# GpSimd's elementwise work given to VectorE and ScalarE: weight splits, the head, the recurrent branch, the gates and the feed-forward products by sevens

## The chip, the cores and the metric

The kernel runs on one core of one Trainium2 chip. The core has TensorE (PE in the profile; PEld is its weight load), VectorE (DVE), ScalarE (ACT), GpSimd (POOL) and SyncE (SP, which here only issues DMAs). The metric is device microseconds for one execution of the whole program: the median of three runs before was 2143.12 us. Lower is better.

## The reference, cut to what matters

One layer of a hybrid decoder trunk on one sequence of 1024 tokens, width 1024, all in float32:

```
h = rmsnorm(x);  proj = h @ w_in                     # 1024 x (2048 + 1544 + 1792 + 3072)
ya = spatial gating MLP (gelu, layernorm, causal mix of 128-token chunks)
yb = forgetting attention (8 heads of 64, softmax with a decay from a cumulated log-sigmoid)
yc = RWKV-7 time mixing (8 heads of 64; token shift, low-rank decay/gates, recurrent state,
     group norm, bonus)
gates = sigmoid(proj[:, gate columns] + bias)        # three of width 1024
x = x + (gates0*(ya@p_a) + gates1*(yb@p_b) + gates2*(yc@p_c)) @ w_out
h = rmsnorm(x);  x = x + (silu(h @ w_gate) * (h @ w_up)) @ w_down      # inner width 2816
out = rmsnorm(x)
```

## The kernel before

**Split products.** Every large matmul is done in a reduced-precision float format by splitting each operand into two tiles: `hi`, a rounded copy that ScalarE writes (`nc.scalar.copy`, a CAST), and `lo`, the remainder `raw - hi` that another engine subtracts. `mm3` (L154 to L158) then issues three matmuls for each block: hi*hi, hi*lo, lo*hi. So each weight tile needs one CAST and one subtraction before the TensorE can use it, and each activation too. The subtraction for weights stands in `w_split` (L134, subtraction on L139); its engine is `low[0]`, which before is GpSimd for the whole program.

**Products by sevens.** Two stages (the gates, about 77 to 325 us of the profile, and the feed-forward up products, about 1530 to 1905 us) use class `Seven` (L317): blocks of a 2x2 product are made from seven products instead of eight (Strassen-Winograd). For each step `f` of such a stage, `begin` does two products from split weights `w_hi`, `w_lo`; `sums` adds and subtracts four quarter blocks of weights on VectorE (L367, L368, L370, L375) and `prepared` (L338) splits five results into `o_hi` (ScalarE, L335) and `o_lo` (GpSimd, L336); `rest` does five more products and adds them up on VectorE (L382 to L390). The activation side is likewise summed and split once, into `T1` to `T4`, `B22` (`T_hi`, `T_lo` of 128x512 each). In the feed-forward stage `act_done` multiplies the two halves of the SwiGLU (L747, GpSimd). All small tiles of a stage share one ring of buffers, `piece` (22 and 25 deep).

**The head** (0 to 77 us) normalises `x` in two halves of 512 tokens, transposes it on TensorE and writes, for the first half, `h_hi` (ScalarE), `h_lo` (VectorE) and their sum `b` (GpSimd, L499, 128x512). For the second half it writes `b` only (ScalarE, L501), forms differences (`t2` and others: L504, L505 on VectorE, L506 and L516 on GpSimd), and splits them into the `T` operands. The first gate products need these operands.

**The recurrent branch** (425 to 875 us) runs eight units of the RWKV recurrence as small dependent steps on all engines (`begin`, `finish`, `chain`); between the steps it places parts of large projections (`projections`, whose weights go through `w_split`) so that TensorE has something to do. A triangular inverse is eliminated in 62 small VectorE instructions in a row for each unit (L1217, L1219). GpSimd does `x_lo`, `y_lo` (L1102, L1206, L1330) and half of `kb` (L1123), besides `w_lo` and some DMA issues.

Then follow attention (to 1200 us; GpSimd makes its bias tiles `lg`, L1481, L1482), the chunk mixing of branch a with the projection of b (to 1275 us; `ya_lo`, `y_lo` on GpSimd), the projection of a (to 1425 us), the output projection and second norm (to 1530 us), the feed-forward up products (to 1905 us) and the down products (to the end; no GpSimd work there).

**What sets the order.** The program's text is handed to a scheduler that places the instructions of each engine in one fixed queue; a queue waits at its head for semaphores and nothing overtakes. Tiles come from pools with a given number of buffers, and a writer waits until the reader of the old content is done.

Of the kernel before, what the change touches and what calls it, by code (L numbers as in the profile page):

```python
# [63 lines left out]
def kernel(ctx: ExitStack, tc: tile.TileContext, a: dict, out: bass.AP):  # L64
# [254 lines left out]
    class Seven:  # L319
# [36 lines left out]

        def sums(self, f, g, scratch=()):
# [9 lines left out]
            nc.vector.tensor_tensor(s1, A21, A22, ALU.add)  # L367
# [91 lines left out]
    fetched.append(gs.fetch(1))
    load_x(1, 4)  # L460
    b11, b21, b12, b22, t2, t3 = ([None] * 4 for _ in range(6))
    for half in range(2):
        xi = x_in[half]
# [14 lines left out]
        for b in (0, 2, 1, 3):  # L478
            for q in range(4):
# [3 lines left out]
                else:  # L483
                    nc.vector.tensor_scalar(xt, xt, r[:, q:q + 1], None, op0=ALU.mult)
        if half == 0:

            ops0 = gs.sums(0, fetched[0][0], [h22_tile(i, F32).rearrange("p (a b) -> p a b", a=4) for i in range(5)])
        for k in range(4):
            for kt in (k, 4 + k):
                ps = xps.tile([P, HALF], F32, name="ps_t", tag="t")  # L490
                for q in range(4):
                    nc.tensor.transpose(ps[:, q * P:(q + 1) * P], xi[q // 2, kt // 2][:, q % 2, (kt % 2) * P:(kt % 2 + 1) * P], ident)
                b = gs.piece("b")
                ((b11, b12), (b21, b22))[kt // 4][half][k] = b
                if half == 0:
                    hi, lo = hh(kt, 0)
                    nc.scalar.activation(hi, ps, AF.Copy, scale=pc("norm_mix", kt))
                    nc.vector.scalar_tensor_tensor(lo, ps, pc("norm_mix", kt), hi.bitcast(F32), op0=ALU.mult, op1=ALU.subtract)
                    nc.gpsimd.tensor_tensor(b, hi.bitcast(F32), lo.bitcast(F32), ALU.add)  # L499
                else:  # L500
                    nc.scalar.activation(b, ps, AF.Copy, scale=pc("norm_mix", kt))  # L501
# [6 lines left out]
        if half == 0:  # L508
            begun = [gs.begin(0, fetched[0])]
            first = [next(ops0)]  # L510
    begun.append(gs.begin(1, fetched[1]))
    for T, src in ((T3, b12), (T1, b11)):
        for k in range(4):
            gs.split(T[k], src[k], nc.vector)
            if T is T3:
                nc.gpsimd.tensor_tensor(b21[k], b21[k], t2[k], ALU.subtract)  # L516
    first += [next(ops0) for _ in range(2)]
# [34 lines left out]
    with ExitStack() as st:  # L552
# [13 lines left out]
        low_rank(1, wts)  # L566
        wa_p, g_p = parts("wa", wa_up, nc.gpsimd), parts("g", g_up, nc.gpsimd)
        for half in range(2):
# [4 lines left out]
            for hp in range(4):  # L573
# [430 lines left out]
def rwkv_branch(tc, a, e):  # L1004
# [4 lines left out]
    with ExitStack() as st:  # L1009
# [67 lines left out]
        def begin(n, u):  # L1077
# [43 lines left out]
            for h, hs in enumerate(heads):  # L1121
                nc.vector.tensor_tensor(kb[hs, :, h, :], v3(k)[hs], v3(pi)[hs], ALU.mult)
                nc.gpsimd.tensor_tensor(kb[hs, :, 1 - h, :], v3(av)[hs], v3(pi)[hs], ALU.mult)  # L1123
            yield 1.5
# [407 lines left out]
```

## Time and profile before

| | before |
|---|---|
| median of three runs (lowest, highest) | 2143.12 us (2140.16, 2145.07) |
| the profiled execution, own time / span | 2139.3 us / 2137.4 us |
| granted TensorE clock, mean | 0.967 |
| busy: PE / DVE / ACT / POOL | 94% / 59% / 41% / 39% |
| largest POOL groups | `w_lo` L139 271.1 us in 114, `o_lo` L336 150.8 us in 105 and 90.5 us in 70 |

In the profile a row of a group reads: line, engine, operation, output<-input, shape, count, busy time in us, mean ns of one, then the idle time of the engine just before them and what ended it. A row of waits reads: who waited, for whom, us in total, how many times, the longest.

### The profile page before, as it was taken

To read this page: it belongs to the slowest core of one execution; us is meant where nothing else is said; L and a number is where in the kernel's file an instruction comes from. 1 tells how busy PE (TensorE), PEld (TensorE's weight loads), DVE (VectorE), ACT (ScalarE), POOL (GpSimd) and SP (SyncE) were. 2 spreads that over 40 slices of the span, in tenths; PEclk is the share of its full clock that TensorE was granted. 3 is DMA by queue.
4 is the path that set the end of the run, shared out by engine and by line. 5 is a ranking of instruction groups with operands and counts; after the bars stand their busy time and mean duration, and the time that the engine had idled before them with its cause. 6 is when DMAs were issued, how large, how long until landed. Compare 5 with 4: busy or idle time off the path is not lost. (4 is left out here: it accounts for less than half of the span.)

```text
span 2137.4 us, 31459 instructions
## 1 busy us (share of the span) xinstructions
PE 2000.8 (94%) x11773; PEld 1598.6 (75%) x11773; DVE 1260.3 (59%) x2398; ACT 882.2 (41%) x1566; POOL 824.2 (39%) x630
## 2 busy tenths in 40 slices
PE   5899999899889899899999989998999999999998
PEld 4688886676777667777666668897778887878886
DVE  8754454777677764245466594436655444556966
ACT  6433335334454454357554322245323222224435
POOL 5654451223232232233444432344676666530000
PEclk8899999899999999999899999999999999999999
DMA  4233335333233322543343753443232332349433
GB/s 124 84 112 116 116 102 195 108 92 107 83 111 93 94 81 80 171 116 99 104 125 102 274 180 99 129 154 98 79 111 90 115 99 91 107 158 327 135 99 123
DMA packets 254700, 260.91 MB, mean 122 GB/s; under 512 B 21430, under 2 KB 195588, under 8 KB 254548
## 3 DMA queue, kind: packets, MB, share of 16 engines
q1 hardware_dynamic: 218388, 208.53, 31.1%
q10 hardware_dynamic: 32928, 41.16, 6.0%
q0 software_dynamic: 3232, 9.21, 1.6%
q8 instruction: 92, 1.51, 0.3%
q14 instruction: 60, 0.49, 0.1%
HBM read 176.77 MB, written 77.89 MB: 119 GB/s over the span
## 5 line engine op out<-in xcount | busy, mean ns | idle before, releaser
L139 POOL TENSOR_TENSOR w_lo<-w_raw,w_hi 128x1024 fp32r<-128x1024 f32 (+2 forms) x114 | 271.1, 2380 | 438.9 <-ACT w_hi L138 438.6
L156 PE MATMUL ps_f<-T_hi,o_hi 128*128 128x512 f32 x576 | 226.7, 394 | 8.4 <-ACT o_hi L335 5.9
L157 PE MATMUL ps_f<-T_lo,o_hi 128*128 128x512 f32 x576 | 227.2, 394 | 7.4 <-DVE T_lo L336 7.4
L158 PE MATMUL ps_f<-T_hi,o_lo 128*128 128x512 f32 x576 | 226.1, 393 | 0.4 <-POOL o_lo L336 0.4
L336 POOL TENSOR_TENSOR o_lo<-s,o_hi 128x512 fp32r<-128x512 f32 x105 | 150.8, 1436 | 85.1 <-ACT o_hi L335 79.1
L138 ACT CAST w_hi<-w_raw 128x1024 fp32r<-128x1024 f32 (+2 forms) x114 | 112.6, 989 | 138.2 <-PE ps_p L157 30.0
L156 PEld LDWEIGHTS ps_f<-T_hi,o_hi 128*128 128x128 f32 x576 | 109.1, 189 | 34.2 <-ACT o_hi L335 6.3
L157 PEld LDWEIGHTS ps_f<-T_lo,o_hi 128*128 128x128 f32 x576 | 109.2, 190 | 32.5 <-DVE T_lo L336 9.4
L158 PEld LDWEIGHTS ps_f<-T_hi,o_lo 128*128 128x128 f32 x576 | 109.3, 190 | 24.0 <-POOL o_lo L336 0.8
L157 PE MATMUL ps_d<-w_lo,a_hi 128*128 128x512 f32 x272 | 106.7, 392 | 1.7 <-DVE w_lo L947 1.7
L158 PE MATMUL ps_d<-w_hi,a_lo 128*128 128x512 f32 x272 | 106.7, 392 | 0.0
L156 PE MATMUL ps_d<-w_hi,a_hi 128*128 128x512 f32 x272 | 104.7, 392 | 0.0
L335 ACT CAST o_hi<-s 128x512 fp32r<-128x512 f32 x105 | 65.0, 619 | 94.2 <-DVE s L368 45.8
L367 DVE TENSOR_TENSOR s<-up_raw 128x512 f32<-128x512 f32 x35 | 27.9, 797 | 126.1 <-DMA up_raw<-in_w_gate_up_dram 118.2
L336 POOL TENSOR_TENSOR o_lo<-up_raw,o_hi 128x512 fp32r<-128x512 f32 x70 | 90.5, 1293 | 27.0 <-ACT o_hi L335 15.6
L375 DVE TENSOR_TENSOR s<-w_raw,s 128x512 f32<-128x512 f32 x35 | 60.3, 1724 | 59.9 <-POOL o_lo L336 59.9
L1481 POOL TENSOR_SCALAR lg<-ck,cq 128x128 f32<-128x128 f32 (+7 forms) x64 | 50.4, 788 | 100.9 <-PE tp L1495 95.5
L871 ACT CAST a_hi<-a_raw 128x1024 fp32r<-128x1024 f32 (+1 forms) x42 | 41.2, 981 | 110.9 <-PE ps_d L157 92.3
L1217 DVE TENSOR_TENSOR tmp<-N,X 128x60 f32<-128x60 f32 (+24 forms) x248 | 77.1, 311 | 9.3 <-DMA N<-nd 1.5
L156 PE MATMUL ps_g<-h_hi,w_hi 128*128 128x512 f32 x192 | 81.6, 425 | 1.0 <-ACT w_hi L138 1.0
L1485 DVE CUSTOM_DVE_ANT_0 lg<-lp,lg 128x128 f32<-128x128 f32 (+7 forms) x64 | 47.9, 753 | 56.2 <-POOL lg L1482 48.6
L158 PE MATMUL ps_g<-h_hi,w_lo 128*128 128x512 f32 x192 | 76.9, 400 | 2.0 <-POOL w_lo L139 2.0
(485 smaller groups left out, 5760.7 us busy)
## 6 DMA issues: line engine op xcount, KB each, us to landing
w_raw<-in_w_in_dram SPq DMA_DIRECT2D x50, 512.0 KB, 4.2
gt<-gate_d ACTq DMA_DIRECT2D x24, 512.0 KB, 3.4
up_raw<-in_w_gate_up_dram SPq DMA_DIRECT2D x44, 256.0 KB, 3.2
w_raw<-in_w_gate_up_dram SPq DMA_DIRECT2D x22, 512.0 KB, 3.9
a_raw<-act_S SPq DMA_DIRECT2D x20, 512.0 KB, 4.1
w<-in_w_down_dram SPq DMA_DIRECT2D x18, 512.0 KB, 6.3
gate_d<-c SPq DMA_DIRECT2D x33, 256.0 KB, 2.1
w_raw<-in_w_out_dram SPq DMA_DIRECT2D x16, 512.0 KB, 5.7
```

The source lines that it names most:

```text
L138: nc.scalar.copy(hi, raw)
L139: low[0].tensor_tensor(lo, raw, hi.bitcast(F32), ALU.subtract)
L156: nc.tensor.matmul(ps, lhs[0], rhs[0], start=first, stop=False)
L157: nc.tensor.matmul(ps, lhs[0], rhs[1], start=False, stop=False)
L158: nc.tensor.matmul(ps, lhs[1], rhs[0], start=False, stop=last)
L335: nc.scalar.copy(dst[0], src)
L336: eng.tensor_tensor(dst[1], src, dst[0].bitcast(F32), ALU.subtract)
L375: nc.vector.tensor_tensor(s4, A12, s2, ALU.subtract)
L871: nc.scalar.copy(hi, raw)
L1217: nc.vector.tensor_tensor(tv, N[:, 0:kx, kx].unsqueeze(1).to_broadcast([P, m, kx]), X[:, i0:8, kx:kx + 1].to_broadcast([P, m, kx]), ALU.mult)
L1481: nc.gpsimd.tensor_scalar(lg[:, 0:nk], ck[h][:, 0:nk], -1.0, cq[:, qb, hd:hd + 1], op0=ALU.mult, op1=ALU.add)
L1485: nc.vector.tensor_tensor_reduce(lg[:, 0:nk], lp[:, 0:nk], lg[:, 0:nk], 1.0, NEG, ALU.add, ALU.max, mx)
```

## The change

All the moved instructions keep their operands; only the engine differs, except in the head.

- `low[0]` is `nc.vector` from the start, so all 114 subtractions `w_lo` run on VectorE, in every stage that uses `w_split` (head, gates, projections in the recurrent branch and attention, the projections of a, b, c, the output projection, the feed-forward).
- The 175 `o_lo` of `prepared`, the 44 products L747, and `x_lo`, `y_lo`, `kb`, `wa_lo`, `g_lo` and the sums L541, L542 run on VectorE.
- In the head L506 and L516 run on VectorE; `b` of the first half is no longer `h_hi + h_lo` on GpSimd but a second scaled copy from PSUM on ScalarE, up to five tiles late; and the second half is normalised ahead of the first gate product in the text.
- GpSimd keeps its DMA issues, `y_lo` of L600, `ya_lo` of L716, the attention bias and a few masks and copies.

```diff
-    low = [nc.gpsimd]
+    low = [nc.vector]
...
-        def prepared(self, src):
+        def prepared(self, src, eng=None):
             o = [self.piece(n, (4, P), F32R) for n in ("o_hi", "o_lo")]
-            self.split(o, src, nc.gpsimd)
+            self.split(o, src, eng or nc.vector)
...
-    for half in range(2):
+    def normed(half):
...
+    def turned(half, xi):
+        plain = []
...
                     nc.vector.scalar_tensor_tensor(lo, ps, pc("norm_mix", kt), hi.bitcast(F32), op0=ALU.mult, op1=ALU.subtract)
-                    nc.gpsimd.tensor_tensor(b, hi.bitcast(F32), lo.bitcast(F32), ALU.add)
+                    plain.append((b, ps, kt))
+                    for b_, ps_, kt_ in [plain.pop(0)] if len(plain) > 4 else []:
+                        nc.scalar.activation(b_, ps_, AF.Copy, scale=pc("norm_mix", kt_))
...
-                nc.gpsimd.tensor_tensor(b12[k], b22[k], b12[k], ALU.subtract)
+                nc.vector.tensor_tensor(b12[k], b22[k], b12[k], ALU.subtract)
...
+    xi0, _ = normed(0)
+    turned(0, xi0)
+    xi1, root = normed(1)
+    ops0 = gs.sums(0, fetched[0][0], [h22_tile(i, F32).rearrange("p (a b) -> p a b", a=4) for i in range(5)], nc.vector)
+    begun = [gs.begin(0, fetched[0])]
+    first = [next(ops0)]
+    turned(1, xi1)
...
-                nc.gpsimd.tensor_tensor(b21[k], b21[k], t2[k], ALU.subtract)
+                nc.vector.tensor_tensor(b21[k], b21[k], t2[k], ALU.subtract)
...
-        nc.gpsimd.tensor_tensor(c, c, kept, ALU.mult)
+        nc.vector.tensor_tensor(c, c, kept, ALU.mult)
...
-            nc.gpsimd.tensor_tensor(hl[1], sq, hl[0].bitcast(F32), ALU.subtract)
+            nc.vector.tensor_tensor(hl[1], sq, hl[0].bitcast(F32), ALU.subtract)
...
-                nc.gpsimd.tensor_tensor(kb[hs, :, 1 - h, :], v3(av)[hs], v3(pi)[hs], ALU.mult)
+                nc.vector.tensor_tensor(kb[hs, :, 1 - h, :], v3(av)[hs], v3(pi)[hs], ALU.mult)
```

Three places in the queues. First, VectorE's queue in the head, where it makes the gate operands (`T20` is the first tile of T2, and so on; `b` and `t2` are the differences). Before:

```order
73 L504 TENSOR_TENSOR b_290<-b_453,b_290 128x512
74 L505 TENSOR_TENSOR t2_462<-b_460,b_290 128x512
75 L504 TENSOR_TENSOR b_308<-b_473,b_308 128x512
76 L336 TENSOR_TENSOR T20_lo_171<-t2_462,T20_hi_170 128x512
77 L505 TENSOR_TENSOR t2_482<-b_480,b_308 128x512
78 L354 TENSOR_TENSOR c11_529<-u_528,ps_f_544 128x512
79 L504 TENSOR_TENSOR b_326<-b_493,b_326 128x512
80 L336 TENSOR_TENSOR T21_lo_173<-t2_482,T21_hi_172 128x512
81 L505 TENSOR_TENSOR t2_502<-b_500,b_326 128x512
82 L336 TENSOR_TENSOR T30_lo_179<-b_453,T30_hi_178 128x512
```

And now the same place in VectorE's queue:

```order
78 L512 TENSOR_TENSOR b_453<-b_460,b_453 128x512
79 L354 TENSOR_TENSOR c11_529<-u_528,ps_f_544 128x512
80 L336 TENSOR_TENSOR T20_lo_171<-t2_462,T20_hi_170 128x512
81 L510 TENSOR_TENSOR b_301<-b_473,b_301 128x512
82 L336 TENSOR_TENSOR T30_lo_179<-b_453,T30_hi_178 128x512
83 L511 TENSOR_TENSOR t2_482<-b_480,b_301 128x512
84 L512 TENSOR_TENSOR b_473<-b_480,b_473 128x512
85 L510 TENSOR_TENSOR b_317<-b_493,b_317 128x512
86 L336 TENSOR_TENSOR T21_lo_173<-t2_482,T21_hi_172 128x512
```

Between the same operands now stand the differences L512 (L506 before), and further on L531 (L516 before) and four `o_lo`: the stretch from the first difference to the last `B22` tile has 41 instructions in place of 29.

Second, VectorE's queue in the recurrent branch, at the end of one unit's preparation (`kb`, `kr`, `r`) and the next step of the state `S`. Before:

```order
622 L1117 SCALAR_TENSOR_TENSOR av_4523<-kap_4655,av_4523 128x512
623 L1122 TENSOR_TENSOR kb_4757<-k_4521,pi_4624 64x8x64 x2
624 L1127 COPY kr_4790<-kap_4655 128x8
625 L1132 SCALAR_TENSOR_TENSOR r_4524<-r_4524,par_65,k_4521 128x256 x2
626 L1310 SCALAR_TENSOR_TENSOR S2_3052<-S1_3051,pd_3473,us_4800 128x64 x2
627 L1321 TENSOR_TENSOR y_lo_4877<-yps_4256,y_hi_4876 128x512
```

And now:

```order
757 L1134 SCALAR_TENSOR_TENSOR av_4523<-kap_4655,av_4523 128x512
758 L1139 TENSOR_TENSOR kb_4757<-k_4521,pi_4624 64x8x64
759 L1140 TENSOR_TENSOR kb_4757<-av_4523,pi_4624 64x8x64
760 L1139 TENSOR_TENSOR kb_4757<-k_4521,pi_4624 64x8x64
761 L1140 TENSOR_TENSOR kb_4757<-av_4523,pi_4624 64x8x64
762 L1144 COPY kr_4790<-kap_4655 128x8
763 L1149 SCALAR_TENSOR_TENSOR r_4524<-r_4524,par_65,k_4521 128x256 x2
764 L139 TENSOR_TENSOR w_lo_4822<-w_raw_4819,w_hi_4821 128x1024
765 L1327 SCALAR_TENSOR_TENSOR S2_3052<-S1_3051,pd_3473,us_4800 128x64 x2
```

The other half of `kb` and one weight subtraction `w_lo` now stand in VectorE's queue ahead of the state's step.

Third, VectorE's queue in one step of the feed-forward products. Before:

```order
1882 L354 TENSOR_TENSOR c11_15674<-u_15673,ps_f_15689 128x512
1883 L382 TENSOR_TENSOR u_15521<-u_15521,ps_f_15734 128x512
1884 L375 TENSOR_TENSOR s2_16007<-w_raw_15814,s2_16007 128x512
1885 L384 TENSOR_TENSOR c21_15748<-u_15521,ps_f_15750 128x512
1886 L386 TENSOR_TENSOR u_15521<-u_15521,ps_f_15764 128x512
1887 L387 TENSOR_TENSOR c22_15749<-c21_15748,ps_f_15764 128x512
```

And now:

```order
2213 L354 TENSOR_TENSOR c11_15674<-u_15673,ps_f_15689 128x512
2214 L139 TENSOR_TENSOR w_lo_15969<-w_raw_15966,w_hi_15968 128x1024
2215 L336 TENSOR_TENSOR o_lo_16011<-s2_16007,o_hi_16010 128x512
2216 L382 TENSOR_TENSOR u_15521<-u_15521,ps_f_15734 128x512
2217 L375 TENSOR_TENSOR s2_16007<-w_raw_15814,s2_16007 128x512
2218 L336 TENSOR_TENSOR o_lo_16016<-up_raw_16002,o_hi_16015 128x512
2219 L384 TENSOR_TENSOR c21_15748<-u_15521,ps_f_15750 128x512
2220 L336 TENSOR_TENSOR o_lo_16020<-s1_16006,o_hi_16019 128x512
2221 L336 TENSOR_TENSOR o_lo_16024<-up_raw_16004,o_hi_16023 128x512
2222 L386 TENSOR_TENSOR u_15521<-u_15521,ps_f_15764 128x512
2223 L387 TENSOR_TENSOR c22_15749<-c21_15748,ps_f_15764 128x512
```

One `w_lo` and the `o_lo` of a later step (`s2_16007` belongs to two steps ahead of `u_15521`) now stand between the additions.

More of the change, by code (lines that the diff above doesn't have):

```diff
@@ L355, in begin, with sums @@
             return g, u, c11
-        def sums(self, f, g, scratch=()):
+        def sums(self, f, g, scratch=(), eng=None):
             c = self.cols(f)[1]
@@ L368, in sums @@
             nc.vector.tensor_tensor(s2, s1, A11, ALU.subtract)
-            yield self.prepared(s2)
+            yield self.prepared(s2, eng)
             nc.vector.tensor_tensor(A21, A11, A21, ALU.subtract)
-            yield self.prepared(A21)
-            yield self.prepared(s1)
-            yield self.prepared(A22)
+            yield self.prepared(A21, eng)
+            yield self.prepared(s1, eng)
+            yield self.prepared(A22, eng)
             s4 = scratch.pop() if scratch else s2
             nc.vector.tensor_tensor(s4, A12, s2, ALU.subtract)
-            yield self.prepared(s4)
+            yield self.prepared(s4, eng)
         def rest(self, f, begun, ops, fps):
@@ L455, in low_rank @@
             carry[n] = shift(ps, ci, half, carry[n], (lw, lg)[n][half])
+    low[0] = nc.vector
     fetched = [gs.fetch(0)]
@@ L460 @@
     load_x(1, 4)
+    low[0] = nc.vector
     b11, b21, b12, b22, t2, t3 = ([None] * 4 for _ in range(6))
-    for half in range(2):
+    def normed(half):
         xi = x_in[half]
@@ L484 @@
                     nc.vector.tensor_scalar(xt, xt, r[:, q:q + 1], None, op0=ALU.mult)
-        if half == 0:
-            ops0 = gs.sums(0, fetched[0][0], [h22_tile(i, F32).rearrange("p (a b) -> p a b", a=4) for i in range(5)])
+        return xi, root
+    def turned(half, xi):
+        plain = []
         for k in range(4):
@@ L505 @@
                 nc.vector.tensor_tensor(t2[k], b22[k], b11[k], ALU.subtract)
-                nc.gpsimd.tensor_tensor(b12[k], b22[k], b12[k], ALU.subtract)
+                nc.vector.tensor_tensor(b12[k], b22[k], b12[k], ALU.subtract)
                 gs.split(T2[k], t2[k], nc.vector)
-        if half == 0:
-            begun = [gs.begin(0, fetched[0])]
-            first = [next(ops0)]
+        for b_, ps_, kt_ in plain:
+            nc.scalar.activation(b_, ps_, AF.Copy, scale=pc("norm_mix", kt_))
+    xi0, _ = normed(0)
[5 more added lines that the diff above has]
+    turned(1, xi1)
     begun.append(gs.begin(1, fetched[1]))
@@ L540 @@
             v, w = gs.piece("v"), gs.piece("w")
-            nc.gpsimd.tensor_tensor(v, hh(k, 0)[0].bitcast(F32), T1[k][0].bitcast(F32), ALU.add)
-            nc.gpsimd.tensor_tensor(w, hh(k, 0)[1].bitcast(F32), T1[k][1].bitcast(F32), ALU.add)
+            nc.vector.tensor_tensor(v, hh(k, 0)[0].bitcast(F32), T1[k][0].bitcast(F32), ALU.add)
+            nc.vector.tensor_tensor(w, hh(k, 0)[1].bitcast(F32), T1[k][1].bitcast(F32), ALU.add)
             nc.vector.tensor_tensor(v, v, w, ALU.add)
@@ L566 @@
         low_rank(1, wts)
-        wa_p, g_p = parts("wa", wa_up, nc.gpsimd), parts("g", g_up, nc.gpsimd)
+        wa_p, g_p = parts("wa", wa_up, nc.vector), parts("g", g_up, nc.vector)
         for half in range(2):
@@ L588 @@
     lrst.close()
+    low[0] = nc.vector
     rwkv_branch(tc, a, locals())
+    low[0] = nc.vector
     lora.close()
@@ L1205, in finish @@
             nc.scalar.copy(hl[0], r)
-            nc.gpsimd.tensor_tensor(hl[1], r, hl[0].bitcast(F32), ALU.subtract)
+            nc.vector.tensor_tensor(hl[1], r, hl[0].bitcast(F32), ALU.subtract)
             yield 1.0
@@ L1329, in chain @@
             nc.scalar.activation(hl[0], y, AF.Square)
-            nc.gpsimd.tensor_tensor(hl[1], sq, hl[0].bitcast(F32), ALU.subtract)
+            nc.vector.tensor_tensor(hl[1], sq, hl[0].bitcast(F32), ALU.subtract)
             yield
```

## The prediction

> **What bounds the kernel now.** I read the profile's page first, then busy times by stage, then what TensorE (PE) waited for in each stage, then the timeline where two engines collide.
>
> ```profile
> span 2137.4 us, 31459 instructions
> PE 2000.8 (94%) x11773; PEld 1598.6 (75%) x11773; DVE 1260.3 (59%) x2398; ACT 882.2 (41%) x1566; POOL 824.2 (39%) x630
> ...
> 15.00:77.00 62.00, 42.26 (x161) 30.83 (x160) 60.39 (x82) 35.89 (x72) 40.25 (x24) 0.81 0.23 67
> 77.00:325.00 248.00, 248.00 (x1080) 202.50 (x1079) 131.24 (x170) 92.61 (x144) 129.05 (x89) 1.00 0.39 113
> 425.00:875.00 450.00, 411.72 (x3968) 318.33 (x3967) 293.38 (x781) 210.32 (x428) 123.39 (x86) 0.96 0.31 93
> 875.00:1200.00 325.00, 305.33 (x1829) 228.32 (x1822) 161.76 (x439) 175.01 (x325) 127.21 (x172) 0.94 0.42 128
> 1200.00:1275.00 75.00, 63.03 (x306) 50.18 (x305) 65.96 (x109) 15.63 (x25) 35.00 (x25) 0.97 0.78 253
> 1425.00:1530.00 105.00, 93.56 (x569) 81.71 (x569) 64.64 (x102) 48.25 (x97) 57.19 (x25) 0.97 0.33 101
> 1530.00:1905.00 375.00, 368.54 (x1598) 300.79 (x1597) 185.94 (x246) 107.79 (x173) 230.43 (x154) 0.99 0.33 107
> ```
>
> The columns of a stretch are its length, then busy us of PE, PEld, DVE, ACT, POOL, then the granted clock. PE is busy 94% of the span. In the gates (77 to 325) it never stops, and in the feed-forward products it stops 6.5 of 375 us, so in these two a cheaper or dearer subtraction moves nothing while DVE keeps up. PE has holes in the head (19.7 us of 62, with the clock at 0.81), in the recurrent branch (38.3 of 450), in attention (19.7 of 325), in the mixing (12.0 of 75) and around the output projection (11.4 of 105). In the head and the mixing DVE is nearly full. What PE waits for there:
>
> ```profile
> PE ps_f L157 <- DVE T_lo L336: 7.4, 4, 3.1
> ...
> PE ps_x L1254 <- ACT M L1247: 7.8, 4, 2.6
> PE zp L1289 <- DVE S L1310: 5.6, 7, 2.1
> PE ps_r L157 <- POOL w_lo L139: 4.6, 2, 3.6
> ...
> PE ps_r L157 <- POOL w_lo L139: 5.3, 4, 1.7
> ...
> PE ps_m L710 <- DVE v L700: 9.9, 15, 1.7
> ...
> PE ps_f L156 <- ACT o_hi L335: 5.9, 1, 5.9
> PE ps_o L157 <- POOL w_lo L139: 3.8, 2, 2.2
> ...
> PE ps_f L156 <- ACT u L353: 6.4, 5, 3.5
> ```
>
> In order these are head, recurrent branch (three), attention, mixing, output projection and its join with the feed-forward (two), feed-forward.
>
> **The price of a moved instruction.** Two pairs of rows from the head's timeline give it (start, length, count):
>
> ```profile
> 58.55 6.78 POOL L336 TENSOR_TENSOR o_lo<-h,o_hi 128x512 fp32r<-128x512 f32 x4 [0.61 <-POOL b L516]
> 67.02 2.90 POOL L139 TENSOR_TENSOR w_lo<-w_raw,w_hi 128x1024 fp32r<-128x1024 f32 x1 [1.69 <-ACT w_hi L138]
> ...
> 59.02 11.45 DVE L336 TENSOR_TENSOR T_lo<-b,T_hi 128x512 fp32r<-128x512 f32 x8
> 70.40 2.48 DVE L336 TENSOR_TENSOR h<-b,h 128x512 fp32r<-128x512 f32 x4
> ```
>
> With POOL idle, four subtractions take 2.48 us, 0.62 each. Beside POOL's rows eight of the same take 11.45 where 4.96 would do: 6.5 us are lost to POOL's four `o_lo` and one `w_lo`, six units of 512 columns, 1.1 each. So the two engines do not run two-operand work side by side here. The loser may be DVE, in instructions of 30 columns, or POOL:
>
> ```profile
> 633.09 2.27 DVE L1217 TENSOR_TENSOR tmp<-N,X 128x30 f32<-128x30 f32 x1
> 635.39 2.29 DVE L1219 TENSOR_TENSOR X<-X,tmp 128x30 f32<-128x30 f32 x1
> 637.72 0.20 DVE L1217 TENSOR_TENSOR tmp<-N,X 128x29 f32<-128x29 f32 x1
> ...
> 632.97 4.66 POOL L139 TENSOR_TENSOR w_lo<-w_raw,w_hi 128x1024 fp32r<-128x1024 f32 x2
> ...
> 1491.34 7.17 POOL L336 TENSOR_TENSOR o_lo<-s,o_hi 128x512 fp32r<-128x512 f32 x1 [13.36 <-ACT o_hi L335]
> 1494.29 3.09 DVE L336 TENSOR_TENSOR T_lo<-bf,T_hi 128x512 fp32r<-128x512 f32 x5
> ...
> L947 DVE TENSOR_TENSOR w_lo<-w,w_hi 128x1024 fp32r<-128x1024 f32 x30 | 36.6, 1221 | 8.0 <-ACT w_hi L946 7.8
> ```
>
> The elimination's steps of 0.20 us took 2.27 and 2.29 behind two `w_lo`; at 1491 one POOL subtraction of 512 columns took 7.17 behind a row of DVE subtractions. A weight subtraction of 1024 columns on DVE costs 1.22 (the down products, no POOL work). So where DVE is full, a moved unit costs 0.62 and gives back about 1.1: a gain of near 0.5. Where DVE is not full it costs PE nothing as long as no wait grows. [...]
>
> **The change part by part.** The terms are changes of the profiled execution, 2139.3 us.
>
> *Head.* Two stretches of it, and the groups that tell what is lost:
>
> ```profile
> 15.30:40.20 24.90, 16.55 (x70) 12.22 (x69) 23.99 (x44) 15.37 (x36) 17.71 (x11) 0.90 0.43 119
> 40.20:72.80 32.60, 21.34 (x80) 15.08 (x78) 32.04 (x29) 19.32 (x34) 22.54 (x13) 0.76 0.11 33
> ...
> L470 DVE CUSTOM_DVE_ANT_0 junk_v<-x_in 128x256 f32<-128x256 f32 x8 | 10.6, 1320 | 0.5 <-DMA x_in<-in_x_dram 0.4
> ...
> 3.78 0.43 DVE L470 CUSTOM_DVE_ANT_0 junk_v<-x_in 128x256 f32<-128x256 f32 x1 [2.75 <-DMA x_in<-in_x_dram]
> ...
> 39.44 0.69 ACT L501 ACTIVATE b<-ps_t,par 128x512 f32<-128x512 f32 x1 [1.07 <-PE ps_t L492]
> ```
>
> From 40.2 to 72.8 DVE is full with 29 instructions of 512 columns; at 0.62 they need 18.0. After, 41 stand there: 25.4 us in place of 32.6, -7.2, if ACT feeds it. From 15.3 to 40.2 the eight square sums lose 8 x (1.32 - 0.43) = 7.1 us; added are two `w_lo` and one `o_lo`, 3.1. That would be -4, but ACT gets eight copies of 0.69 (5.5 us) where `h_hi` also comes from, so I take -3. PE's last products hang on the last `B22` tile before and after. Head: -10, between 0 (ACT becomes the limit) and -15.
>
> *Gates.* 14 steps of five `o_lo` and one `w_lo` add 70 x 0.62 + 14 x 1.22 = 61 us to DVE's 131 of 248: 192, still below PE, whose work hides it. The queue shows the `o_lo` placed ahead by about two steps. 0 (0 to +3). 325 to 425, with a few moved units: -1 (-3 to +2).
>
> *Recurrent branch* (first two rows) *and attention* (the third).
>
> ```profile
> L139 POOL TENSOR_TENSOR w_lo<-w_raw,w_hi 128x1024 fp32r<-128x1024 f32 (+1 forms) x24 | 57.8, 2409 | 140.6 <-ACT w_hi L138 140.4
> L1123 POOL TENSOR_TENSOR kb<-av,pi 64x512 f32<-64x512 f32 x14 | 22.9, 1638 | 84.6 <-DVE av L1117 84.0
> ...
> L139 POOL TENSOR_TENSOR w_lo<-w_raw,w_hi 128x512 fp32r<-128x512 f32 (+1 forms) x15 | 26.8, 1789 | 42.7 <-ACT w_hi L138 42.6
> ```
>
> 24 `w_lo`, 14 `kb` and three `x_lo`/`y_lo` for each of seven units are 83 units of 512 columns: +51 us on DVE at 0.62, up to 83 x 1.1 = 91 given back. Net between +51 and -40 us of DVE time, of which only what lies on the unit's chain reaches PE; DVE is busy 293 of 450. The longest block of a chain step falls from two `w_lo` (2.3 each) to 1.22. The wait of PE for `w_lo` (4.6) should halve. Added is a hazard: `w_lo` waits for ACT and a DMA at the head of DVE's queue, ahead of the state's step. I take -7 (+10 to -25).
>
> *Attention*: the four waits for `w_lo` (5.3) shorten by 4 x (2.4 - 1.2) = 4.8, less what DVE's queue adds: -3 (+5 to -8). `lg` on POOL no longer queues behind `w_lo`. *Mixing*: eight `w_lo` of one unit each on a full DVE: 8 x (0.62 - 1.1) = -4 (0 to -10); `ya_lo` stays on POOL. *Output projection and join*: two waits for `w_lo`, -2; the 5.9 us hole came from the 7.17 us subtraction, which now takes its turn, while DVE gets three `o_lo` and a `w_lo` (3.1) in front of the last operands: -4. Together -6 (0 to -10). *Feed-forward*: 22 steps of five `o_lo`, one `w_lo` and two products add 154 x 0.62 + 22 x 1.22 = 122 us to DVE's 186 of 375, if all lay in the stretch: 308 at most, below PE. PE's five waits (6.4) came through `u`, freed by L747: -2 (+6 to -8). The down products have no POOL work: 0. SP and POOL keep their DMA issues; these wait for buffers that DVE now frees.
>
> Sum: -10 - 1 - 7 - 3 - 4 - 6 - 2 = -33. 2139.3 - 33 = 2106.3. The profiled execution lies 3.8 below the median of 2143.1, so 2110.
>
> **The rivals.** *Hidden anyway:* PE is the bound, and only the two places where DVE alone feeds it pay, the head and the join: -16, 2127. Speaking for it: PE is 94% busy. Against: the rows of 2.27 us in a chain on which PE waits. [...]
>
> *More than that:* the recurrent branch gives -25 and attention -8, as the holes there (38.3 and 19.7) close and the clock (0.96 and 0.94) rises with them: -33 - 18 - 5 = -56, 2087.
>
> *Slower:* the queue of DVE. Before, POOL idled at the head of its queue:
>
> ```profile
> POOL w_lo L139 <- ACT w_hi L138: 438.6, 90, 20.1
> ...
> ACT w_hi L138 <- DMA w_raw<-in_w_in_dram: 9.8, 4, 3.6
> ...
> DVE s L367 <- DMA up_raw<-in_w_gate_up_dram: 118.2, 20, 14.3
> ```
>
> 438.6 us in 90 waits cost nobody, as nothing urgent stood behind. On DVE the state's step or the softmax stands behind. DVE already waits 5.9 us on average for `up_raw` in the feed-forward, so the order in the queue can be wrong about a DMA. There are 24 + 15 `w_lo` in the recurrent branch and attention. The other terms sum to -23; at 23/39 = 0.6 us of PE time lost for each, the gain is gone. At 1.2 us each: +47 - 23 = +24, 2167. Against it: the order puts `w_lo` where `w_hi` is expected to be done, and ACT itself waited only 9.8 us for `w_raw` of the input projection.
>
> **How the numbers follow.** Forecast 2110 (own range 2098 to 2121) 0.38; hidden anyway 0.24; more 0.18; gains and queue waits cancelling 0.07; slower 0.13. Faster by over 0.2% (4.3 us, about what a measurement can tell from no change) is then 0.38 + 0.24 + 0.18 = 0.80. The range 2085 to 2148 leaves out part of the second and most of the last case.
>
> **What would show it.** Right: DVE busy for less than 1260 plus the moved units at 0.62, and its two-operand groups near the single price; L470 at 0.43; PE full from near 67 in place of 77; no DVE row of 30 columns above 0.3 us outside the copies of POOL; the hole at 1493 gone; DVE's sum below 308 in the feed-forward. Wrong: ACT with waits of DVE behind it in the head; waits of DVE for `w_hi` in the recurrent branch of over 20 us in all; new holes of PE behind DVE's `o_lo` in the gates.

## The result, and the profile after

The changed kernel takes 2069.84 us (median of four runs, 2068.17 to 2072.46) against 2141.64 us of the kernel before in the same comparison: ratio 0.9666, 95% interval 0.9645 to 0.9687, or 71.8 us less. The forecast was 33 us less, with 2085 us as the low end of the range. The direction was right, the size was missed by more than half. One execution in the tables below (3502.13 us, of rec_wlo, at a granted clock of 0.82) is left out of its ratio. The profiled executions compare 2070.7 us of span with 2137.4. From the page of the changed kernel (line numbers are up to 17 higher than before):

```profile
span 2070.7 us, 31190 instructions
...
PE 1981.1 (96%) x11773; PEld 1589.2 (77%) x11773; DVE 1396.1 (67%) x2794; ACT 896.9 (43%) x1576; POOL 163.1 (8%) x226
...
L139 DVE TENSOR_TENSOR w_lo<-w_raw,w_hi 128x1024 fp32r<-128x1024 f32 (+2 forms) x114 | 135.2, 1187 | 76.0 <-ACT w_hi L138 74.1
...
L336 DVE TENSOR_TENSOR o_lo<-s,o_hi 128x512 fp32r<-128x512 f32 x105 | 72.3, 688 | 18.9 <-PE ps_f L157 11.7
```

These two groups alone are 207.5 us of work that VectorE did not have before, and there are more, yet its busy time rose by only 135.8 (1260.3 before). The rest was given back by instructions that are no longer held. For every VectorE instruction I took its duration less the shortest of the same form (operation, tiles and shape) in that trace, below called its held time; summed, this is 217 us before and 55 after.

Where the 67 us of the two traces lie follows from the start of the same matmul in both: the head ends 12.1 us earlier, the gates add 0.0, 325 to 390 3.7, the recurrent branch 26.2, attention, mixing and the projections up to the output projection 7.5, the join with the feed-forward 6.4 and the feed-forward behind it 11.7; the down products take 0.9 more. The stages after, cut at the same matmuls, in the columns of the prediction:

```profile
0.00:65.00 65.00, 42.43 (x174) 30.08 (x175) 54.59 (x131) 47.27 (x102) 3.96 (x12) 0.89 0.39 114
65.00:313.00 248.00, 248.00 (x1080) 202.47 (x1079) 166.15 (x265) 97.81 (x149) 1.65 (x3) 1.00 0.38 115
373.00:794.00 421.00, 400.47 (x3834) 312.97 (x3830) 309.75 (x902) 205.50 (x420) 25.61 (x29) 0.96 0.34 101
1152.00:1226.00 74.00, 61.60 (x308) 50.70 (x307) 64.81 (x113) 15.07 (x24) 26.17 (x17) 0.95 0.75 244
1376.00:1480.00 104.00, 98.27 (x588) 85.63 (x587) 79.00 (x134) 49.52 (x98) 0.00 (x0) 0.98 0.37 113
1480.00:1849.00 369.00, 369.00 (x1623) 304.50 (x1623) 271.69 (x407) 114.76 (x173) 0.00 (x0) 1.00 0.35 113
```

The recurrent branch between the same matmuls before:

```profile
389.00:836.00 447.00, 406.86 (x3839) 316.73 (x3837) 316.06 (x843) 205.06 (x420) 122.67 (x87) 0.95 0.32 95
```

PE's holes there fell from 40 to 20.5 us and its busy time from 406.9 to 400.5 for the same matmuls, while VectorE's busy time hardly changed: it took over POOL's 97 us at the price of what it got back. The feed-forward has no hole left (369.00 of 369.00).

### The profile page after: what moved, and what is told of

Its sections match the earlier page's. It is cut to its first block, busy times and chain, and to the rows that moved or that the text cites. A ratio compares the mean times of both kernels' runs of the same rounds, so it can differ in the third digit from the quotient of the medians.

```text
span 2070.7 us, 31190 instructions
## 1 busy us (share of the span) xinstructions
PE 1981.1 (96%) x11773; PEld 1589.2 (77%) x11773; DVE 1396.1 (67%) x2794; ACT 896.9 (43%) x1576; POOL 163.1 (8%) x226
## 5 line engine op out<-in xcount | busy, mean ns | idle before, releaser
L139 DVE TENSOR_TENSOR w_lo<-w_raw,w_hi 128x1024 fp32r<-128x1024 f32 (+2 forms) x114 | 135.2, 1187 | 76.0 <-ACT w_hi L138 74.1
L336 DVE TENSOR_TENSOR o_lo<-s,o_hi 128x512 fp32r<-128x512 f32 x105 | 72.3, 688 | 18.9 <-PE ps_f L157 11.7
L157 PE MATMUL ps_g<-h_lo,w_hi 128*128 128x512 f32 x192 | 75.8, 395 | 0.0
L157 PE MATMUL ps_o<-w_lo,m_hi 128*128 128x256 f32 x256 | 73.4, 287 | 2.4 <-DVE w_lo L139 2.4
L158 PE MATMUL ps_o<-w_hi,m_lo 128*128 128x256 f32 x256 | 73.2, 286 | 0.0
L1513 ACT COPY PT<-tp 128x512 f32<-128x512 f32 (+3 forms) x96 | 45.6, 475 | 62.7 <-PE tp L1512 62.3
L156 PE MATMUL ps_o<-w_hi,m_hi 128*128 128x256 f32 x256 | 72.7, 285 | 0.0
```

Source lines behind the costliest of these rows:

```text
L139: low[0].tensor_tensor(lo, raw, hi.bitcast(F32), ALU.subtract)
L156: nc.tensor.matmul(ps, lhs[0], rhs[0], start=first, stop=False)
L157: nc.tensor.matmul(ps, lhs[0], rhs[1], start=False, stop=False)
L158: nc.tensor.matmul(ps, lhs[1], rhs[0], start=False, stop=last)
L336: eng.tensor_tensor(dst[1], src, dst[0].bitcast(F32), ALU.subtract)
L1513: nc.scalar.copy(PT[h][k0 // 4][:, 0:n, qi * P:(qi + 1) * P], tp[:, 0:n, :])
```

## The experiments

Each was timed in five rounds beside the kernel before. "Against the changed kernel" is the difference of the two ratios times 2142 us; with 0.2% on each ratio such a difference is uncertain by about 6 us. Stage times are from one profiled execution each; most untouched stages differed by 1 to 2 us between executions, but attention took between 355 and 364 us, and the recurrent branch was once (ff_all) 8 us shorter.

| kernel | median us | ratio to before (95%) | against the changed kernel |
|---|---|---|---|
| rec_wlo | 2091.82 | 0.9753 (0.9725 to 0.9781) | +19 |
| rec_small | 2075.51 | 0.9681 (0.9656 to 0.9706) | +3 |
| rec_both | 2102.23 | 0.9809 (0.9785 to 0.9834) | +31 |
| rec_twin | 2113.10 | 0.9862 (0.9838 to 0.9886) | +42 |
| rec_zero | 2073.64 | 0.9680 (0.9659 to 0.9701) | +3 |
| ff_olo | 2072.91 | 0.9672 (0.9653 to 0.9691) | +1 |
| ff_prod | 2074.94 | 0.9680 (0.9658 to 0.9701) | +3 |
| ff_wlo | 2071.04 | 0.9656 (0.9635 to 0.9676) | -2 |
| ff_olo_prod | 2073.17 | 0.9671 (0.9644 to 0.9697) | +1 |
| ff_all | 2085.07 | 0.9726 (0.9709 to 0.9743) | +13 |
| ff_twin | 2103.06 | 0.9813 (0.9791 to 0.9834) | +31 |
| head_pool | 2070.85 | 0.9657 (0.9639 to 0.9675) | -2 |
| more | 2075.94 | 0.9682 (0.9661 to 0.9703) | +3 |
| lg_act | 2084.24 | 0.9723 (0.9704 to 0.9741) | +12 |
| wlo_only | 2090.93 | 0.9749 (0.9730 to 0.9768) | 54 less than before |
| head_order | 2139.62 | 0.9979 (0.9965 to 0.9994) | 4.5 less than before |
| order_wlo | 2080.21 | 0.9718 (0.9697 to 0.9739) | 60 less than before |

**The recurrent branch: whose work, and why.** My theory A was that GpSimd's subtractions hold VectorE's small instructions. Rivals: PE waits for the late results themselves (B), or the unit's own small operations became shorter (C).

```diff
 rec_wlo (from the changed kernel)
-    low[0] = nc.vector
+    low[0] = nc.gpsimd
     rwkv_branch(tc, a, locals())
```

> The changed kernel, with the weight subtractions w_lo of the recurrent branch's projections back on GpSimd (24 of 1024 columns, some of 512); x_lo, y_lo and kb stay on VectorE. Theory A (shared access: while GpSimd subtracts, VectorE's small chain instructions are held; 58.7 us of excess on VectorE in this stage before, 11.7 after): w_lo was 58 to 70 of GpSimd's 110 us there, so a bit over half of the 26 us return: +14 us, 2084. Theory B (PE only waits for the late result itself): its waits for w_lo were 4.6 + 2.0 us: +4 us, 2074. Theory C (what helped was that the small operations of the unit's chain got shorter, w_lo has no part): 0, 2070.

```diff
 rec_small (at x_lo, y_lo of the branch, and the second half of kb)
-            nc.vector.tensor_tensor(hl[1], sq, hl[0].bitcast(F32), ALU.subtract)
+            nc.gpsimd.tensor_tensor(hl[1], sq, hl[0].bitcast(F32), ALU.subtract)
```

> The changed kernel, with x_lo (two places), y_lo and half of kb of the recurrent branch back on GpSimd; w_lo stays on VectorE. Theory A (shared access): about 45 of GpSimd's 110 us: +10 us, 2080. Theory B (late w_lo): 0. Theory C (the chain's own small operations): these stand in the unit's chain with up to 1.6 us each for kb and 1 to 2 for x_lo and y_lo, and nearly all 26 us return: 2090 to 2096.

The edit of rec_both is the two together.

> The changed kernel with w_lo, x_lo, y_lo and kb of the recurrent branch all back on GpSimd. By every theory the whole 26 us of this stage return: 2096 (2090 to 2100). Less than 20 would say that part of the gain in this stage came from the stages before it (where the stage starts relative to its DMAs), not from its own instructions.

Putting back w_lo costs 19 us, the small operations 3, both 31 (26 expected). Between the same matmuls the branch takes 420.1 us as changed, 436.0, 424.2 and 441.2. B falls: PE waits 4.5 us for `w_lo` in rec_wlo and 3.5 as changed, 1 us of the 16. C falls: kb and x_lo were in the chain, but they are worth 3 to 4 us. What PE waits for longer is the state's step `S`. As changed, then in rec_wlo:

```profile
PE zp L1306 <- DVE S L1327: 0.6, 1, 0.6
```

```profile
PE zp L1306 <- DVE S L1327: 8.5, 8, 2.2
```

And what grows in VectorE's queue is the elimination, 62 small instructions in a row per unit. Its two groups in this stage before:

```profile
L1217 DVE TENSOR_TENSOR tmp<-N,X 128x60 f32<-128x60 f32 (+24 forms) x248 | 77.1, 311 | 9.3 <-DMA N<-nd 1.5
L1219 DVE TENSOR_TENSOR X<-X,tmp 128x60 f32<-128x60 f32 (+24 forms) x248 | 68.3, 275 | 8.1
```

and in the changed kernel:

```profile
L1234 DVE TENSOR_TENSOR tmp<-N,X 128x60 f32<-128x60 f32 (+24 forms) x248 | 60.5, 244 | 7.9 <-DMA N<-nd 0.6
L1236 DVE TENSOR_TENSOR X<-X,tmp 128x60 f32<-128x60 f32 (+24 forms) x248 | 52.4, 211 | 7.5
```

145.4 us against 112.9. With w_lo alone back on GpSimd the sum is 140.8 (84.1 and 56.7), with the small operations alone 118.5. The direct test lets GpSimd repeat the work for nobody:

```diff
 rec_twin (in w_split, during the recurrent branch)
         low[0].tensor_tensor(lo, raw, hi.bitcast(F32), ALU.subtract)
+        if twin[0]:
+            nc.gpsimd.tensor_tensor(twin[0].tile([P] + shape, mybir.dt.bfloat16, name="twin", tag="twin", bufs=1), raw, hi.bitcast(F32), ALU.subtract)
```

> The changed kernel, and GpSimd does every w_lo of the recurrent branch a second time into a tile that nobody reads (bf16 output, since no more room was left). No result of the program comes from GpSimd there; only its presence is added. Theory A (shared access): as much as putting w_lo back on GpSimd costs, +10 to +16 us, VectorE's 30-column steps again at about 2.3 us beside it and its excess in the stage up from 12 to over 35 us. Theories B and C: 0 to +3 us (w_raw is held a little longer).

It costs 42 us, far more than the 10 to 16 expected, and no result of the branch's `w_lo` comes from GpSimd. VectorE's timeline (start, length, count), with GpSimd's row of the same stretch last:

```profile
687.10 0.19 DVE L1240 TENSOR_TENSOR X<-X,tmp 128x31 f32<-128x31 f32 x1
687.33 2.27 DVE L1238 TENSOR_TENSOR tmp<-N,X 128x30 f32<-128x30 f32 x1
689.52 1.21 DVE L140 TENSOR_TENSOR w_lo<-w_raw,w_hi 128x1024 fp32r<-128x1024 f32 x1
690.65 0.18 DVE L1240 TENSOR_TENSOR X<-X,tmp 128x30 f32<-128x30 f32 x1
...
687.14 2.40 POOL L142 TENSOR_TENSOR twin<-w_raw,w_hi 128x1024 bf16<-128x1024 f32 x1 [3.60 <-issue]
```

GpSimd starts at 687.14 and ends at 689.54; the step of 30 columns that starts within ends with it, 2.07 us longer than its neighbours. GpSimd has 23 such rows in the stage, and 18 VectorE instructions are held so, most by 2.0 to 2.2 us: 14 steps of the elimination, a `kb`, a `w_lo` and two scalings of a single input tile. The elimination's groups are again at 78.1 and 62.9, 141.0 together. The run is dearer than rec_wlo by 23 us; VectorE also does its own 24 subtractions there (24 x 1.21 = 29), which is about the size, and one wait of PE for `w_lo` itself, 7.3 us, is part of it. The windows of rec_both (441.2) and rec_twin (460.1 between the same matmuls) show it on PE too, the latter with the clock at 0.91:

```profile
373.00:817.00 444.00, 400.46 (x3812) 311.36 (x3813) 320.45 (x851) 204.68 (x418) 126.02 (x89) 0.96 0.32 96
```

```profile
373.00:834.00 461.00, 413.59 (x3810) 321.46 (x3811) 348.33 (x908) 205.09 (x420) 90.79 (x52) 0.91 0.31 92
```

The control: GpSimd present, but reading nothing.

```diff
 rec_zero (in w_split, during the recurrent branch)
+            for _ in range(2):
+                nc.gpsimd.memset(lo.bitcast(F32), 0.0)
         low[0].tensor_tensor(lo, raw, hi.bitcast(F32), ALU.subtract)
```

> The changed kernel, and GpSimd writes zeros twice into each w_lo tile of the recurrent branch before VectorE writes it, reading nothing; VectorE's subtraction waits for that. Control to the twin run, which cost 42 us. If any work of GpSimd beside VectorE costs: +20 us or more, elimination steps of about the length of the zeroing again. If only GpSimd's reading holds VectorE: 0 to +4 us, no elimination step above 0.5 us beside the zeroing.

+3 us, inside the uncertainty. Beside 1.97 us of zeroing (two rows joined) the elimination goes on at its own pace, and its groups take 60.4 and 52.2 us in the stage, 60.5 and 52.4 as changed:

```profile
729.31 0.24 DVE L1239 TENSOR_TENSOR tmp<-N,X 128x48 f32<-128x48 f32 x1
729.59 0.21 DVE L1241 TENSOR_TENSOR X<-X,tmp 128x48 f32<-128x48 f32 x1
729.83 0.25 DVE L1239 TENSOR_TENSOR tmp<-N,X 128x49 f32<-128x49 f32 x1
730.11 0.21 DVE L1241 TENSOR_TENSOR X<-X,tmp 128x49 f32<-128x49 f32 x1
...
729.52 1.97 POOL L142 MEMSET w_lo<- 128x1024 f32 x2 [12.05 <-PE ps_g L162]
```

So in these runs it is not GpSimd's being busy, nor its writing, that holds the elimination: the GpSimd subtraction of 2.40 us above, which reads two tiles of SBUF, holds one VectorE instruction for 2.07 us, nearly its whole span. That fits the reading as the cause; the two runs do not separate it from anything else in which a subtraction differs from a zeroing.

**The feed-forward and its join.**

```diff
 ff_olo: self.split(o, src, nc.vector) of the feed-forward's prepared -> nc.gpsimd
 ff_prod, in act_done
-        nc.vector.tensor_tensor(c, c, kept, ALU.mult)
+        nc.gpsimd.tensor_tensor(c, c, kept, ALU.mult)
 ff_wlo, where the feed-forward begins
+                low[0] = nc.gpsimd
                 ready = [fs.begin(0)]
 ff_olo_prod: the first two.  ff_all: all three.
```

> The changed kernel, with the o_lo of the feed-forward's sevens (110) back on GpSimd; w_lo and the products stay on VectorE. The join and the feed-forward gave 18 us in the changed kernel (8 foreseen). Theory D (the ring of pieces: late o_lo hold the pieces, up_raw comes late, VectorE stands at L367 for 104 us behind that DMA with the sums of PE's next step queued behind it): +10 to +18, 2080 to 2087, VectorE's wait for up_raw back above 60 us. Theory E (the product on GpSimd held u): 0 to +3. Theory A (held instructions on VectorE alone): +3, since VectorE has room.

> The changed kernel, with the 44 products of the feed-forward (silu half times the other half) back on GpSimd; o_lo stays on VectorE. Theory D: 0 to +2. Theory E (PE's five waits of 6.4 us came through u, which the product frees): +6 to +11, with the waits of PE for u back. Theory A: 0 to +1.

Theory E missed: in ff_prod PE has no hole behind the join (369.00 busy of 369.00). Theory D missed too. VectorE's wait for `up_raw` does come back, 85.8 us after 8.9 in the changed kernel, first row of the changed kernel, second of ff_olo:

```profile
DVE s L367 <- DMA up_raw<-in_w_gate_up_dram: 8.9, 13, 2.0
```

```profile
DVE s L367 <- DMA up_raw<-in_w_gate_up_dram: 85.8, 18, 7.4
```

but PE does not notice it:

```profile
1480.00:1849.00 369.00, 369.00 (x1623) 304.45 (x1622) 246.70 (x313) 112.29 (x177) 144.82 (x99) 1.00 0.36 114
```

What o_lo costs lies in the join, where the profile of ff_olo shows PE waiting for it once, and the join is 5.7 us longer than as changed:

```profile
PE ps_f L158 <- POOL o_lo L336: 7.6, 1, 7.6
```

The median saw only +1 of these; the trace of that execution +5.4 in all.

> The changed kernel with the feed-forward's w_lo alone on GpSimd (22 of 1024 columns). Theory G (w_lo is what the feed-forward's 11 us hang on): +8 to +12, 2080. Theory F (all three together make GpSimd's queue the path; busy 237 of 387 before, about 55 here): 0 to +2, 2071.

> The changed kernel, with o_lo and the products of the feed-forward back on GpSimd, w_lo on VectorE. Each alone left PE without a hole in the stage (369 of 369 us). Theory F (GpSimd's queue is the path: the product waits behind o_lo and w_lo, and u behind the product): holes behind u come back in part, +6 (join) and 4 to 8: 2080 to 2085. Theory G (w_lo of 2.4 to 2.8 us on GpSimd is what is missing): join alone, +6.

> The changed kernel, with o_lo, the products and w_lo of the feed-forward all back on GpSimd: the stage as it was before. If the stage's own instructions explain its gain: +17 us, 2087 (6 of them in the join, as o_lo alone cost there, and 11 behind it), with PE's holes behind u back and the clock at half speed after them. If part of the gain came from elsewhere (a different place of the DMAs after the earlier stages): +6 to +10.

Each alone and o_lo with the products cost at most 1 us behind the join, so theory G missed. All three cost 11.9 there, and 13 in the whole (17 expected), with PE's waits for `u` back:

```profile
PE ps_f L156 <- ACT u L353: 7.3, 7, 3.7
```

The same from the other side: wlo_only, below, frees only `w_lo` and gains 10.8 there. So it was the load of GpSimd's queue as a whole (233 us busy of 387 before), and it is enough to take `w_lo` off it, or the other two. Theory F is the nearest, though it expected 4 to 8 us already from o_lo and the products; through which of the queue's waits the path goes was not isolated.

```diff
 ff_twin (in prepared of the feed-forward)
             self.split(o, src, nc.vector)
+            nc.gpsimd.tensor_tensor(self.twin.tile([P, 4, P], mybir.dt.bfloat16, name="twin", tag="twin", bufs=1), src, o[0].bitcast(F32), ALU.subtract)
```

> The changed kernel, and GpSimd does nearly every o_lo of the feed-forward a second time into a tile that nobody reads (bf16 output). Theory A (presence alone costs): each span of 1.3 us that meets VectorE at work holds it once; VectorE is busy 272 of 369, so some 80 of 105 meet it: its busy sum rises by about 80 to 350, still below PE: 0 to +4; past 369 it would be +10 or more. Theory D: a piece is held until the second reading is done, as before the change: +6 to +18 with waits for up_raw. Theory E: 0.

+31: far over what I expected of any theory. VectorE's busy time was to rise by 80 and stay below PE's. It did stay below (327 of the stage's 397 us, 272 of 369 as changed; held time 62.6 us after 2.6), and yet PE has 20 holes of 0.3 to 2.9 us behind `u` and `c`, 18 us in all, nearly one at every step. So an engine that is busy 82% of a stretch delayed one that had no hole without it; that this comes from work in bursts was not tested. VectorE's wait for `up_raw` is 41.8 us here, as theory D has it, but 85.8 us of it in ff_olo left PE without a hole, so it is not enough by itself.

**The head.**

```diff
 head_pool (changed kernel): L512, L531, the five o_lo and two w_lo of the head on nc.gpsimd
 head_order (kernel before): only normed/turned, i.e. the new order and b as ScalarE's copy
```

> The changed kernel, with the head's w_lo (two), the five o_lo of the first step, and the differences L512 and L531 back on GpSimd; the order of the text and the copy of b on ScalarE stay as changed. Theory A (VectorE is full there and held once for each span of GpSimd): the head lost 9 to 12 us by the whole change; nearly all returns: +7 to +10. Rival (the gain is the new order of the text, and ScalarE's copy of b): 0 to +3.

> The kernel before with the head's new text only: the second half normalised ahead of the first gate product, and b as ScalarE's copy; every subtraction and product stays on GpSimd (L512, L531, o_lo and w_lo too). If the order and the copy are the head's gain: -8 to -11 us against before, 2132. If the engine moves of the head are: 0 to -3, 2140.

By the median the rival was right for head_pool: -2, no loss, though 10 of VectorE's rows of 512 columns there are about 1.7 us again in place of 0.69. Its trace says a little more: the head is 1.7 us longer than in most executions, and the gates behind it 2.0 (250.0 in place of 248.0), 3 to 5 us in all, which the uncertainty of the medians hides; theory A wanted 7 to 10. Up to the end of the head VectorE is busy 54.2 us with this work on GpSimd (0 to 68) and 54.6 with it on VectorE (0 to 65): what is given back and what is added nearly cancel. The new text alone ends the head 7.5 us earlier in its trace and the gates 5.2, and the whole kernel keeps about 4.5. w_lo alone (below) ends the head 6.6 earlier and the gates 4.9, the two 11.6 and 10.7, the whole change 12.1 and 12.0.

**The two parts that carry it.**

```diff
 wlo_only (kernel before)
-    low = [nc.gpsimd]
+    low = [nc.vector]
 order_wlo: that and head_order
```

> The kernel before with all 114 w_lo on VectorE and nothing else changed. By the price found in the recurrent branch (putting w_lo back there cost 19 us) -19 there, -4 in attention, -4 in the mixing and the output projection, -5 in the feed-forward: -32, 2110. If o_lo and the small operations, left on GpSimd, hold VectorE all the more now that it has more to do: -10, 2132.

> The kernel before with the head's new text (order, b on ScalarE) and all 114 w_lo on VectorE; o_lo, the products, x_lo, y_lo, kb and the head's differences stay on GpSimd. If the two parts add up: -54 - 5 = -59 against before, 2085; the other 360 moved instructions are then worth 13 us, 6 of them o_lo in the join and 3 to 4 the small operations of the recurrent branch. If they overlap in the head, where both gain 7 us: -54, 2090.

The 114 `w_lo` alone bring 54 of the 72 us, 22 more than I expected even after the runs above: 21.8 in the recurrent branch, 10.8 in the feed-forward, 6.6 in the head (of which the gates lose 1.7 again), about 7 from attention to the projection of a, 5.1 between 325 and 390. Its one trace is 49 us shorter than that of before; 54 is by the ratio. With the head's new text it is 60, so the two add up. GpSimd lost 404 instructions in all (630 to 226): the 114 `w_lo`, eight sums that the new text replaces, and 282 others (the expectation's 360 was a miscount). The 282 are worth about 11.

**Further in the same direction.**

```diff
 more, in y_split and in the mixing: y_lo and ya_lo from nc.gpsimd to nc.vector
 lg_act, attention's bias
-  nc.gpsimd.tensor_scalar(lg[:, 0:nk], ck[h][:, 0:nk], -1.0, cq[:, qb, hd:hd + 1], op0=ALU.mult, op1=ALU.add)
+  nc.scalar.activation(lg[:, 0:nk], ck[h][:, 0:nk], AF.Identity, scale=-1.0, bias=cq[:, qb, hd:hd + 1])
```

> The changed kernel, and y_lo (8 of 1024 columns) and ya_lo (16 of 512) of the attention's end and the mixing also on VectorE. There VectorE is busy 65 of 74 us and held 14 us by GpSimd. Theory A by the measured price (a span held once, less the own time): 14 us come off and 20 us are added, the latter partly outside the mixing: -4 to +4. If whole spans count on PE's path as in the recurrent branch: -8. If VectorE's own time counts: +5.

> The changed kernel with the 64 bias tiles L1498 of attention on ScalarE (Identity with scale -1 and the bias column) in place of GpSimd; the masking L1499 stays. VectorE is held 19.5 us there by GpSimd, ScalarE is busy 195 of 358. Theory A: up to half of the 19.5 us is L1498's and PE's waits there (15 us) close in part: -2 to -6, 2066. Rival: ScalarE's chain (exponential, copies of PT on which PE waits 2.7 us) gets 32 us longer: +3 to +10.

Neither helps. In `more` the held time of the mixing fell from 14.1 to 1.5 us and VectorE's own work took its place (68.6 us busy in the stage's 81, after 64.8 in 74); the subtraction that PE needs now queues behind others. As changed, then in `more`:

```profile
PE ps_p L158 <- DVE w_lo L139: 5.5, 4, 2.3
```

```profile
PE ps_p L158 <- DVE w_lo L139: 13.2, 5, 4.6
```

In lg_act the rival was nearest: VectorE's held time in attention did fall, from 19.5 to 9.3 us, but ScalarE is busy 242 us there in place of 195 and PE's waits for `PT` are 7.3 us after 2.7. These waits are only part of the 12 us. No version tried beats the changed kernel beyond the uncertainty.

## Why the prediction was right or wrong

- *The price.* A unit of 512 columns on GpSimd was said to take 1.1 us from VectorE and to cost 0.62 there. Measured in the recurrent branch: a `w_lo` of two units that hits holds one instruction 2.07 us, and it costs 1.21. This step held, for those that hit: 18 of 23 in rec_twin.
- *The recurrent branch, -7 (to -25); measured -26 (rec_both, which undoes it, loses 21 in the stage and 31 by the median of the whole).* This is the term that failed, in the step "only what lies on the unit's chain reaches PE ... I take -7". It netted 51 us added against up to 91 given back over the whole stage and took a small share. VectorE's net was small indeed: it is busy 6 us less. But the two sides do not count alike for PE. The trace of before could have told where the hits lie: 37 of the stage's 59 us of held time were in the elimination, on which the unit's next steps wait. After the change it is 4 of 12, so 33 us left this row of steps, and PE gained 26. The added instructions cost PE much less than their length. rec_wlo shows it: it takes 29 us of own time off VectorE and adds 34 us of held time, nearly nothing net, and PE loses 16; rec_small adds 18 us of held time, only 5 of it in the elimination, and PE loses 4. How the delay goes on from the elimination to PE is read from the program and these sums; it was not followed row by row. A price of 24 `w_lo` x (2.07 - 1.21) = 21 comes near the 16 (rec_wlo) and 22 (wlo_only) of this stage, partly by luck, since not every `w_lo` hits and the 1.21 does not count in full.
- *The feared queue.* VectorE waited 6.6 us in four waits for `w_hi` in the recurrent branch (sign of "wrong": over 20). The slower rival did not come about there; it shows in small in the mixing of `more`.
- *Feed-forward, -2 (to -8); measured -11.7.* The second term that failed. PE's waits (6.4 us) were followed to `u` and from there to the product alone, which by itself is worth nothing (ff_prod); what counted was the load of GpSimd's whole queue. And a hole was priced at its own length, while the one of 3.5 us before had a clock of 0.50 behind it (1590 to 1595), as the last section shows.
- *Join and output projection, -6; measured about -6.* The hole of 5.85 that began at 1493 became two of 1.39 and 1.56; the cause named (o_lo of 7.17 us on GpSimd) is what ff_olo brought back.
- *Head, -10; measured -12 in the two traces, about -11 against the other executions.* The size was right, the reason half wrong: the sum took 7.2 from units given back on a full VectorE, but by head_pool these are worth 3 to 5 at most, and nothing by its median. The new text, costed at nothing by itself, and `w_lo` carry the rest. The foreseen gain at L470 came: 0.42 us after 0.87.
- *Gates, 0; measured 0.0.* VectorE 166 of 248, PE without a hole. *325 to 425, -1; measured -3.7 to 390*, mostly from `w_lo` (wlo_only -5.1). *Attention -3 and mixing -4; measured about -7.5 together*, of which attention about 5, the mixing 2 and the projection of a 1. Right as a sum, not in its parts.
- *The clock.* Span times (1 - mean granted clock) is 2137.4 x 0.033 = 71 us before and 2070.7 x 0.026 = 54 after, so by this estimate up to 17 of the 67 us are matmuls that no longer run at the lower clock (0.50 in the rows of the last section). PE's busy time for the same 11773 matmuls fell by 19.7. The prediction named this only in its rival of -56.

The rivals: hidden anyway (-16) is excluded, slower too. "More than that" gave the recurrent branch its size (-25) and was still too small in the whole, above all since it left the feed-forward at -2.

## What to carry to other kernels

Engine totals did not price the work moved off GpSimd here: VectorE's net in the recurrent branch was 6 us, PE's gain 26. Look for the chain of short VectorE instructions on which TensorE waits (here the elimination: 37 of the stage's 59 us of held time before, 4 of 12 after), count how many of its rows have about the length of a GpSimd subtraction beside them (2.27 beside 2.40 us in rec_twin), and charge those in full. Take the largest operands first: 114 of 404 moved instructions carried 54 of 72 us. Stop where VectorE is itself full: in the head (busy 54.2 us of 68 with this work on GpSimd, 54.6 of 65 with it on VectorE) and in the mixing (64.8 of 74, then 68.6 of 81 in `more`) the time given back and the time added nearly cancelled.

## What the runs showed of the hardware

In rec_twin a GpSimd subtraction of 2.40 us held a two-operand VectorE instruction that came after it, one of 30 columns, for nearly its whole span (2.07 us). In rec_zero GpSimd writing zeros for 1.97 us held none of the elimination's (0.21 to 0.25 us beside it). The zeroing did hold four scalings and copies of VectorE that read a single tile, by 0.6 to 0.8 us.

A hole of 3.52 us in PE cost more than its own length. In the kernel before at 1585 (columns as above, the clock is the third value from the end), and PE's own rows:

```profile
1585.00:1590.00 5.00, 1.48 (x5) 0.96 (x4) 3.78 (x7) 2.76 (x4) 1.58 (x1) 0.81 0.13 50
1590.00:1595.00 5.00, 5.00 (x13) 3.84 (x13) 2.68 (x4) 1.68 (x4) 4.91 (x3) 0.50 0.45 163
1595.00:1600.00 5.00, 5.00 (x24) 4.11 (x23) 3.47 (x5) 1.15 (x2) 4.11 (x4) 1.00 0.36 105
```

```profile
1584.99 0.39 PE L157 MATMUL ps_f<-B_lo,o_hi 128*128 128x512 f32 x1
...
1589.12 0.79 PE L156 MATMUL ps_f<-B_hi,w_hi 128*128 128x512 f32 x1 [3.52 <-ACT u L353]
...
1592.70 0.63 PE L158 MATMUL ps_f<-B_hi,w_lo 128*128 128x512 f32 x1
1593.13 0.63 PE L156 MATMUL ps_f<-B_hi,w_hi 128*128 128x512 f32 x1
```

Matmuls follow each other at 0.43 us in place of 0.23 for about 5.5 us, 13 of them: some 2.6 us on top of the hole. Behind a hole of 1.70 us at 1881.7 the clock stays at 1.00 (1882 to 1905). But it is not the length of the hole alone. In the same trace a hole of 1.75 us, in the mixing, has half the clock behind it:

```profile
1271.06 1.91 PE L710 MATMUL ps_m<-wsT,v 128*128 128x128 f32 x6 [1.75 <-DVE v L700]
...
1273.62 0.63 PE L158 MATMUL ps_p<-y_hi,w_lo 128*128 128x512 f32 x1
1274.04 0.63 PE L156 MATMUL ps_p<-y_hi,w_hi 128*128 128x512 f32 x1
```

```profile
1270.70:1277.50 6.80, 6.44 (x18) 5.20 (x19) 4.54 (x9) 2.80 (x4) 2.35 (x3) 0.50 0.49 155
```

All changes of the clock in this trace lie on one grid with a step of 3.41 us (1270.70, 1277.53, 1588.14 and 1594.97 among them), so where a hole falls on the grid may matter too; what decides was not worked out. Between the first two of these and between the last two it is 0.50:

```profile
1270.70:1277.53 6.83, 6.47 (x18) 5.23 (x19) 4.54 (x9) 2.83 (x4) 2.38 (x3) 0.50 0.49 155
1588.14:1594.97 6.83, 5.84 (x14) 4.59 (x15) 4.09 (x6) 3.19 (x5) 5.19 (x4) 0.50 0.43 156
```
